# Down projection of 16 hidden tiles in seven-product blocks, on one core

## The chip, the cores and the metric

The kernel runs on one core of a Trainium2 chip. The metric is the device time of one execution in microseconds. The kernel before takes 649.57 us (median of 3 runs, 649.49 to 649.74).

## The reference

Two groups of rows, 512 of a new stream and 64 of a running one, go through one layer of a hybrid encoder: a state-space part and a latent-attention part side by side, an output projection, then a dense SwiGLU network. The change touches only the last of these:

```python
x = x + jnp.concatenate([y_ssd, o], axis=-1) @ p['w_out']
hf = rmsnorm(x, p['norm_ffn'])
x = x + (jax.nn.silu(hf @ p['w_gate']) * (hf @ p['w_up'])) @ p['w_down']
...
y_prompt = rmsnorm(xp, norm_final)
```

All values are float32. The model width is 1024, the hidden width of the SwiGLU network is 2816, and the 576 rows of both groups share the weights.

## The kernel before

The data is held transposed: channels on the 128 partitions, the 576 rows along the free axis. The model width is 8 tiles of 128 channels (`x2[0]` to `x2[7]`), the hidden width 22 tiles. A product runs over 288 rows (`TH`), half of them.

**Precision.** Every float32 operand is split into a high part in a format that TensorE multiplies at its full rate and a low part that is the rest: ScalarE writes the high part (`act.copy`), VectorE the low one (a subtraction), see `split_weights` and `split_scaled`. A product is then three: high x high, high x low, low x high.

**Gate and up, `gu_weights`, `gu_steps`, `gu_first`.** For one hidden tile f the gate and up products form a 2 x 2 block scheme: two row halves on one side, gate and up on the other, even and odd channel tiles as the inner pair. Seven block products take the place of eight. This needs sums of the weights (four additions of 512 columns on VectorE: `s1`, `s2`), three splits of 1024 columns and one of 512 (`a22`), and sums of the activations, which `x_operands` makes once. The seven products are the steps `m1` to `m7`; they accumulate in three PSUM banks `x`, `y`, `z`. `m1` is copied by ScalarE into `gl` and added to `y` by VectorE in `m2`. The steps `m4` and `m3` of one tile are issued after `m1` of the next (`late`). `finish` applies silu, multiplies gate and up into `u`, and splits `u` into `prod[f]`.

**Down, `down`, `down_terms`, `down_half`.** The hidden tiles are cut by `CUTS` into parts 0-4, 5-9, 10-13, 14-17 and 18-21. After the first tile of a part the part before goes through `down`: for each of the 8 output tiles and each half of the rows, its hidden tiles are multiplied by their weights in one PSUM bank, and VectorE adds the bank to `x2[t]`. In the first part `x2[t]` is multiplied by `Ri` before, the inverse of the norm's factor per row, so that the norm can be left to the end. The last part goes through the tail of the kernel, with the final norm.

**What sets the order.** Every engine's instructions are issued in an order written out by hand in `ISSUE`, a list of places for each engine. What moves between engines goes by semaphores. Buffers come from rotating pools: `wpool` (8) for raw weights and their sums, `w2pool` (10) for split weights, `tpool` (7) for temporaries such as `g` and `u`, PSUM banks by tag (`sc` 3, `pp` 3, `hm` 2). SP's queue loads all weights.

Of the kernel before, what the change touches and what calls it, by code (L numbers as in the profile page):

```python
# [11 lines left out]
F32 = mybir.dt.float32  # L12
F32R = mybir.dt.float32r
AF = mybir.ActivationFunctionType
ALU = mybir.AluOpType
# [4 lines left out]
P = 128  # L20
# [3 lines left out]
T = TP + TS  # L24
# [11 lines left out]
UPW = 3 + TP + 3 + TS  # L36
LAST = 18


# [15 lines left out]
def hybrid_layer_kernel(ctx: ExitStack, tc: tile.TileContext, a, o):  # L55
# [49 lines left out]
    def wslot(wp, name, dt=F32):  # L105
        return wp.tile([P, 1024], dt, tag="w", name=name)
# [26 lines left out]
    def wk(w, k, m=P):  # L133
        return tuple(z[:, k * m : (k + 1) * m] for z in w)
# [646 lines left out]
    fz = midp.tile([P, 4, T], F32, tag="xsd", name="fz")  # L781
    ss2, ss3 = fz[:, 0], fz[:, 1]
    R2, R2h = R1, R1h
# [22 lines left out]

    def gu_weights(f):

        r1, r2, s1, s2 = (wslot((w2pool, wpool)[f > 0], f"gu{f}_{z}") for z in range(4))
        sp.dma_start(r2, a["w_gu"][f, :, 1])  # L810
        gu_dma.append(sp.dma_start(r1, a["w_gu"][f, :, 0]).ins)
        l, r = (lambda z: z[:, :512]), (lambda z: z[:, 512:])
        dve.tensor_tensor(l(s1), l(r2), r(r2), ALU.add)
        dve.tensor_tensor(l(s2), l(r2), l(r1), ALU.subtract)
        dve.tensor_tensor(r(s1), l(s1), l(r1), ALU.subtract)
        dve.tensor_tensor(r(s2), r(r1), r(s1), ALU.subtract)
        a22 = wslot(w2pool, f"gu{f}_a22", F32R)
        act.copy(l(a22), r(r2))
        out = {"A22": (l(a22), r(a22))}
        for names, w in (("A11", "A12"), r1), (("S1", "S2"), s1), (("S3", "S4"), s2):  # L820
            w = split_weights(w, f"gu{f}_{names[0]}", wp=w2pool)
            for i, n in enumerate(names):
                out[n] = tuple(z[:, 512 * i : 512 * i + 512] for z in w)
        dve.tensor_tensor(r(a22), r(r2), l(a22).bitcast(F32), ALU.subtract)
        return out

    w_gu, squared, gu_dma = {}, [], []

    def square(t):
# [20 lines left out]
    def block_product(ps, w, i, kps=KPS, first=True, last=True, onto=False):  # L850

        n, xi = PRODUCTS[i - 1]
        for kp in kps:
            (whi, wlo), x = wk(w[n], kp), xops[kp][:, :, xi]
            for j, (p, q) in enumerate(((whi, x[:, 0]), (whi, x[:, 1]), (wlo, x[:, 0]))):
                pe.matmul(  # L856
                    ps, p, q, start=not onto and first and kp == kps[0] and j == 0,
                    stop=onto or (last and kp == kps[-1] and j == 2), skip_group_check=onto,
                )
# [4 lines left out]

    prod, Ri = {}, fz[:, 2]
    HC = [slice(hf * TH, (hf + 1) * TH) for hf in range(2)]

# [34 lines left out]
    def finish(f, g, u):  # L902
        act.activation(g, g, AF.Silu)
        dve.tensor_tensor(u, u, g, ALU.mult)
        s = slot(cpool, "c", f"pr{f}")
        split_scaled(s, u, None)
        prod[f] = hilo(s)

    def gu_steps(f):
# [7 lines left out]
        def m1():  # L917
            block_product(x, w, 1)
            act.copy(gl, x)

# [8 lines left out]
        def m2():  # L929
            block_product(y, w, 2)  # L930
            dve.tensor_tensor(gl, y, gl, ALU.add)
            dve.tensor_tensor(gl, gl, R2[:, :TH], ALU.mult)

# [14 lines left out]

    wout[0] = w2pool

    def down_terms(fs, t):
# [10 lines left out]
    def down(fs):  # L962

        for t in range(KT):
            terms = down_terms(fs, t)
            for hf, cols in enumerate(HC):
                ps = fbank(("hm", "sc", "pp")[(2 * t + hf) % 3], f"ps_d{fs[0]}_{t}")
                down_half(ps, terms, cols)
                if fs[0] == 0:
                    dve.tensor_tensor(x2[t][:, cols], x2[t][:, cols], Ri[:, cols], ALU.mult)  # L970
                dve.tensor_tensor(x2[t][:, cols], ps, x2[t][:, cols], ALU.add)
# [167 lines left out]
def issue_in_order(tc, nc):  # L1139
# [25 lines left out]
1190-1192 1227 1193-1198 1291-1297 1199-1201 1228 1202-1204 1286-1288 1207-1223 1318-1319 1224-1226 1298-1317  # L1165
1330-1333 1342-1343 1348-1355 1344-1347 1320-1329 1334-1341 1356-1463 1572 1464-1499 1575 1500-1523 1581-1582
1524-1554 1573-1574 1555-1558 1560-1571 1559 1583 1578-1580 1599-1601 1620 1584-1586 1605-1607 1626 1576-1577
1596-1598 1590-1592 1611-1613 1632-1634 1621 1587-1589 1608-1610 1602-1604 1623-1624 1593-1595 1614-1616 1635-1637
1629-1631 1617-1619 1638 1627-1628 1647 1622 1641-1643 1658 1656 1653-1655 1648 1625 1644 1659 1639-1640 1649-1651
1645-1646 1660-1669 1657 1682 1652 1694-1705 1683-1693 1670-1681 1730-1741 1706-1710 1718-1729 1711-1717 1754-1765  # L1170
1742-1753 1766-1777 1790-1801 1778-1789 1802-1825 1850 1862-1873 1838-1839 1826-1837 1840-1849 1851-1861 1874-1909
1922-1932 1910-1921 1934 1946-1957 1933 1935-1945 1958-1969 1982-1993 1970-1981 1994-2030 2042-2065 2093-2094
2031-2041 2095-2096 2078-2091 2097-2106 2066-2077 2108-2114 2107 2092 2115-2117 2123-2137 2118-2122 2138
""",
# [11 lines left out]
365 336 325 337 321 331 333 366 341 340 338 332 334 346 345 342 335 339 344 349 352 358 343 350 377 359 347 351 368  # L1186
353 360 354 361 356 355 348 357 369-373 376 374 390 375 382 378 383-384 389 379 385-387 380 397 405 381 388 391 394
393 398 395 392 399 401 420 396 402-403 400 406 404 408 407 462 412 409-410 417 464 414 418 416 413 421 411 423 422
419 424-425 428 426-427 415 431 429 432-433 430 463 434 438 436 435 437 442 465 439 443 441 440 466 444 451 446 467
452 468 453 447 454-455 469 473 456 475 477 448 457 474 478 476 458 472 488 470 479 481 445 489-490 449 492 480 471  # L1190
495 491 538 450 485 459 493 487 460 494 482 500 507 503 486 505 461 497 508 504 506 502 510 496 501 518 509 483
519-520 570 521 484 548 515 555 511 522-523 517 524 516 545 526 512 498 537 525 527 513 499 542 528-529 514 532 565
547 573 563 533 560 552 543 557 562 577 530 540 558 539 568 579 550 534 541 531 580 575 553 544 549 535 578 546 551
567 572 554 588 556 584 589-590 559 581 561 591 564
""",
# [8 lines left out]
230 225 272 237-239 236 245 251 246 252 248 278 247 255 254 249-250 232 257-259 256 261 253 262-264 268-270 260  # L1204
265-267 273-276 284 277 280-282 285 293 287 283 279 286 288 291 289 302 290 292 294-296 330 298 300 297 301 303-304
299 305-307 309-310 308 312 331 311 316-317 313 315 314 318 332 319 333 320 322 321 337-338 323-325 334 336 335 326
339 327 341 340 346 344 347 345 348-350 328 355-356 329 353-354 357 359 358 342-343 364 362 365-366 363 367-368 351
375 352 376 371 360 372 369 361 370 377-380 373 381-386 390 374 391 387 389 392 388 394 393 399 397 400 395 398 401
396 402-403 408-409 406 404 407 405 410-412 417-418 413 415-416 414 419-421 428-429 422 424-425 423 430-432 426
433-439 443 427 444 440 442 445 441 447 446 452 450 453 448 451 454 449 455-456 461-462 457 459-460 458 463-465  # L1210
472-473 466 468 467 469 474-477 470 478 471 479-483 487-488 484 486 489 485 491 490 496 494 497 492 495 498 493
499-500 505-506 501 503-504 502 507-509 516-517 510 512 511 513 518-521 514 522 515 523-527 531-532 528 530 533 529
535 534 540 538 541 536 539 542 537 543-544 552-553 547 545 548 546 554-555 549-551 556
""",
    "POOL": """
0-3 7 18 28 4 8 5 9 6 10 26-27 11 29 12-17 20-22 19 23-25 31 30 32-42 53 55 57 59 54 56 58 60 43-52 61-73
# [3 lines left out]
83 70 74 67 69 68 71 78 80 88 73 75 72 66 89 77 76 82 86 90-92 87 93 100 103 101-102 104-105  # L1220
""",
# [100 lines left out]
```

## Time and profile before

| | |
|---|---|
| median of 3 runs | 649.57 us |
| span of the profiled execution | 647.9 us |
| TensorE (PE) busy | 639.4 us, 4747 products |
| VectorE (DVE) busy | 510.1 us |
| ScalarE (ACT) busy | 338.3 us |
| GpSimd (POOL) busy | 43.2 us |
| DMA | 63.22 MB, mean 98 GB/s |

The profiled execution's own time is not among the runs; its span runs from its first to its last instruction. The feed-forward stage begins near 250 us, the old down projections are pieces of the chain such as 321.90, 409.55, 485.67 and 555.78 us, and the last part with the final norm begins near 606 us. In a row, L856 is the seven-product scheme, L958 the plain down projection, L112 and L113 the two halves of a weight split, L813 to L816 the weight sums. The rows give busy time, the mean length of one instruction, and the idle time of the engine in front of it with what ended it.

### The profile page before, as it was taken

What the parts mean: (1) busy time and instruction counts of PE and PEld (TensorE: products, weight loads), DVE (VectorE), ACT (ScalarE), POOL (GpSimd) and SP (SyncE); (2) the same over time, 40 slices, a digit from 0 to 9 for tenths busy, and PEclk for the clock granted to TensorE, in tenths of its full rate; (3) what the DMA queues carried; (4) which work ended last, traced back from release to release, by engine and by line L of the source; (5) the groups of instructions that cost most, each with busy time, mean ns of one, the idle gap of its engine ahead of it and who ended that gap; (6) DMA issues with size and microseconds to landing.
All of it is one profiled execution on the core that took longest, in us unless ns stands there. A gap on an engine that the chain in (4) does not pass through costs nothing.

```text
span 647.9 us, 11907 instructions
## 1 busy us (share of the span) xinstructions
PE 639.4 (99%) x4747; PEld 613.0 (95%) x4747; DVE 510.1 (79%) x932; ACT 338.3 (52%) x629; POOL 43.2 (7%) x79
## 2 busy tenths in 40 slices
PE   9999999999999999999999999999999999999996
PEld 9799999886887899999999999999999999999995
DVE  6999986999767699999895876866767676966555
ACT  7645425879666467745523455234533254335364
POOL 1422131101100000000000000000000000000022
PEclk9999999999999999999999999999999999999998
DMA  9521273313220221233322133122223223231004
GB/s 317 192 82 46 64 208 119 111 52 122 111 71 33 99 98 66 78 119 109 120 96 98 66 102 126 67 72 75 83 98 126 70 82 105 75 130 66 1 1 147
DMA packets 26151, 63.22 MB, mean 98 GB/s; under 512 B 3418, under 2 KB 10088, under 8 KB 25840
## 3 DMA queue, kind: packets, MB, share of 16 engines
q1 hardware_dynamic: 24560, 60.77, 28.0%
q0 software_dynamic: 816, 1.13, 0.7%
q8 instruction: 37, 0.61, 0.4%
q10 hardware_dynamic: 720, 0.57, 0.3%
q14 instruction: 18, 0.15, 0.1%
HBM read 58.03 MB, written 3.30 MB: 95 GB/s over the span
## 4 chain that ended last, share of the span: by engine, by line
PE 92%; DVE 4%; issue 1%; ACT 1%; DMA 1%; POOL 0%; POOLq 0%; DVEq 0%; ACTq 0%
PE ps_x L856 21%; PE ps_d L958 18%; PE ps_z L856 10%; PE ps_o L447 8%; PE ps_in L128 8%; PE ps_y L856 5%; PE ps_z L447 4%; PE ps_l L958 3%; PE ps_first L128 2%; PE ps_p L856 2%; PE sc L661 2%; PE pv L708 1%; PE ptp L683 1%; PE ps_v L594 1%; DVE mx L644 1%
## 5 line engine op out<-in xcount | busy, mean ns | idle before, releaser
L958 PE MATMUL ps_d<-pr,wh_d 128*128 128x288 f32 x576 | 115.6, 295 | 0.0
L856 PE MATMUL ps_x<-xop,wh_gu_S 128*128 128x288 f32 x504 | 101.5, 295 | 0.0
L958 PEld LDWEIGHTS ps_d<-pr,wh_d 128*128 128x128 f32 x576 | 92.6, 188 | 0.0
L958 PE MATMUL ps_d<-pr,wl_d 128*128 128x288 f32 x288 | 84.7, 295 | 0.0
L856 PEld LDWEIGHTS ps_x<-xop,wh_gu_S 128*128 128x128 f32 x504 | 80.8, 188 | 0.0
L856 PE MATMUL ps_x<-xop,wl_gu_S 128*128 128x288 f32 x252 | 74.3, 295 | 0.0
L112 ACT CAST wh_gu_S<-gu 128x1024 fp32r<-128x1024 f32 x44 | 46.2, 1050 | 39.9 <-PE ps_d L958 18.5
L113 DVE TENSOR_TENSOR wl_gu_S<-gu,wh_gu_S 128x1024 fp32r<-128x1024 f32 x44 | 53.8, 1223 | 9.0 <-PE ps_d L958 6.7
L958 PEld LDWEIGHTS ps_d<-pr,wl_d 128*128 128x128 f32 x288 | 54.1, 188 | 0.0
L856 PEld LDWEIGHTS ps_x<-xop,wl_gu_S 128*128 128x128 f32 x252 | 47.3, 188 | 0.0
L128 PE MATMUL ps_in<-xs,wh_in 128*128 128x288 f32 x256 | 45.4, 298 | 0.0
L112 ACT CAST wh_d<-wr_d 128x640 fp32r<-128x640 f32 (+1 forms) x32 | 21.5, 673 | 45.6 <-PE ps_x L856 20.4
L128 PEld LDWEIGHTS ps_in<-xs,wh_in 128*128 128x128 f32 x256 | 37.8, 189 | 0.2
L856 PE MATMUL ps_z<-xop,gu_a 128*128 128x288 f32 x252 | 37.5, 295 | 0.0
L856 PE MATMUL ps_y<-xop,wh_gu_A 128*128 128x288 f32 x168 | 35.4, 295 | 0.0
L856 PE MATMUL ps_z<-xop,wh_gu_S 128*128 128x288 f32 x168 | 35.2, 297 | 0.0
L113 DVE TENSOR_TENSOR wl_d<-wr_d,wh_d 128x640 fp32r<-128x640 f32 (+1 forms) x32 | 24.1, 756 | 13.7 <-PE ps_x L856 8.6
L856 PEld LDWEIGHTS ps_z<-xop,gu_a 128*128 128x128 f32 x252 | 34.9, 189 | 0.0
L856 PE MATMUL ps_x<-xop,wh_gu_A 128*128 128x288 f32 x168 | 34.7, 297 | 0.0
L112 ACT CAST wh_gu_A<-gu 128x1024 fp32r<-128x1024 f32 x22 | 23.1, 1050 | 21.2 <-PE ps_x L856 13.1
L113 DVE TENSOR_TENSOR wl_gu_A<-gu,wh_gu_A 128x1024 fp32r<-128x1024 f32 x22 | 27.0, 1227 | 6.9 <-PE ps_d L958 4.1
L1054 POOL TENSOR_TENSOR fz<-fz,sq 128x320 f32<-128x320 f32 x3 | 2.6, 882 | 445.7 <-ACT sq L1049 445.7
(337 smaller groups left out, 1646.9 us busy)
## 6 DMA issues: line engine op xcount, KB each, us to landing
gu<-in_w_gu SPq DMA_DIRECT2D x44, 512.0 KB, 3.7
wr_d<-in_w_down SPq DMA_DIRECT2D x16, 320.0 KB, 3.0
wr_in<-in_w_in SPq DMA_DIRECT2D x8, 512.0 KB, 5.9
wr_out<-in_w_out SPq DMA_DIRECT2D x8, 512.0 KB, 3.2
wr_d<-in_w_down SPq DMA_DIRECT2D x16, 256.0 KB, 2.6
cumb<-cumD SPq DMA_DIRECT2D x5, 512.0 KB, 4.3
x<-in_xT SPq DMA_DIRECT2D x2, 1152.0 KB, 6.5
wr_z<-in_w_in SPq DMA_DIRECT2D x4, 512.0 KB, 4.4
```

Of the source, the lines that this page charges most:

```text
L112: act.copy(hi, raw)
L113: dve.tensor_tensor(lo, raw, hi.bitcast(F32), ALU.subtract)
L128: pe.matmul(ps[:m, hf, :n], w, x[:, hf * n : (hf + 1) * n], start=start and k == 0 and i == 0, stop=stop and k == last and i == 2,)
L447: pe.matmul(ps[:, :n], w, x[:, cols], start=k == 0 and i == 0, stop=k == len(terms) - 1 and i == 2,)
L594: pe.matmul(ps[:n], l, r, start=j == 0, stop=j == 2)
L644: dve.tensor_reduce(mx[:, j : j + 1], s, AX, ALU.max, negate=True)
L661: pe.matmul(s[:, :nk], qs[:, j, q0 : q0 + P], ks[:, j, :nk], start=True, stop=True)
L683: pe.transpose(pp[:, k : k + P], prs[p, i][:, j, b * P : b * P + P], ident)
L708: pe.matmul(pv[64 * j : 64 * j + 64, b * P :], V[b][:, h * HD : (h + 1) * HD], pts[p, b, j], start=b == 0, stop=True, skip_group_check=b > 0,)
L856: pe.matmul(ps, p, q, start=not onto and first and kp == kps[0] and j == 0, stop=onto or (last and kp == kps[-1] and j == 2), skip_group_c ...
L958: pe.matmul(ps, w, x[:, cols], start=first and k == 0 and i == 0, stop=last and k == len(terms) - 1 and i == 2,)
L1054: pool.tensor_tensor(ss3[:, parts[0]], ss3[:, parts[0]], z, ALU.add)
```

## The change

The hidden tiles are cut into parts 0-1, 2-5, 6-9, 10-13, 14-17 and 18-21. Parts 0-1 and 18-21 stay plain. The four parts between go through the seven-product scheme for the down projection too: pairs of output tiles, pairs of hidden tiles and the two row halves form the blocks. Each part is done in two calls of `down_blocks`, each for four output tiles, one behind each of the first two hidden tiles of the next part. `gu_weights` becomes `block_weights`, which both stages use, with its sums on VectorE; `pair` makes the sums and splits of the activations for two hidden tiles. In both stages `m1` is copied by ScalarE from its bank into the bank of `m2`, which accumulates on it. Of each pair of output tiles, the even one is added by VectorE from PSUM; the odd one is copied to buffers `B` and `C` by ScalarE and added to `x2` by two accumulating DMAs from GpSimd's queue. The multiplication of `x2` by `Ri` moves from VectorE (16 of 288 columns) to GpSimd (8 of 576). `ss3` gets a pool of its own, and the five lists of `ISSUE` are written anew from the feed-forward stage on.

```diff
+BLOCKS = tuple(range(2, LAST + 1, 4))
...
     def gu_weights(f):
+        return block_weights(*(a["w_gu"][f, :, i] for i in range(2)), f"gu{f}", lambda z: z.rearrange("p (e b m) -> e p b m", e=2, m=P))
+    def down_weights(f, h):
+        src = a["w_down"][4 * h : 4 * h + 4, :, f * P : f * P + 512].rearrange("(t i) k c -> i k t c", i=2)
+        return block_weights(src[0], src[1], f"db{f}_{h}", lambda z: z.rearrange("p (b e m) -> e p b m", e=2, m=P))
...
+    def block_weights(src1, src2, name, blocks):
+        n = len(gu_dma)
+        sums = dve
+        r2, r1, s1, s2 = (wslot((w2pool, wpool)[n > 0], f"{name}_{z}") for z in range(4))
...
+        sums.tensor_tensor(l(s1), l(r2), r(r2), ALU.add)
+        sums.tensor_tensor(l(s2), l(r2), l(r1), ALU.subtract)
+        sums.tensor_tensor(r(s1), l(s1), l(r1), ALU.subtract)
+        sums.tensor_tensor(r(s2), r(r1), r(s1), ALU.subtract)
+        a22 = wslot(w2pool, f"{name}_a22", F32R)
         act.copy(l(a22), r(r2))
...
     def finish(f, g, u):
         act.activation(g, g, AF.Silu)
         dve.tensor_tensor(u, u, g, ALU.mult)
+        if BLOCKS[0] <= f < LAST:
+            return paired(f, u)
...
         def m1():
             block_product(x, w, 1)
-            act.copy(gl, x)
+            act.copy(y, x)
...
         def m2():
-            block_product(y, w, 2)
-            dve.tensor_tensor(gl, y, gl, ALU.add)
-            dve.tensor_tensor(gl, gl, R2[:, :TH], ALU.mult)
+            block_product(y, w, 2, onto=True)
+            dve.tensor_tensor(gl, y, R2[:, :TH], ALU.mult)
...
+    def pair(f):
...
+        x, y = (halves(tmp(f"pv{f}_{i}")) for i in range(2))
+        dve.tensor_tensor(x[:, 0], e[:, 1], e[:, 0], ALU.subtract)
+        dve.tensor_tensor(x[:, 1], e[:, 1], d[:, 1], ALU.subtract)
+        dve.tensor_tensor(y[:, 0], d[:, 1], x[:, 0], ALU.subtract)
+        dve.tensor_tensor(y[:, 1], d[:, 0], y[:, 0], ALU.subtract)
+        for z, v in ((a11, e[:, 0]), (own, d), (t13, x), (t24, y)):
+            zr = z.bitcast(F32R)
+            act.copy(zr[:, 0], v)
+            dve.tensor_tensor(zr[:, 1], v, z[:, 0], ALU.subtract)
...
+    def down_steps(fs, w, h, p):
+        t = 4 * h + 2 * p
+        qs = blocks[(fs[0] - BLOCKS[0]) // 2 :][:2]
+        x, y, z = fbank("hm", f"ps_dx{fs[0]}_{t}"), fbank("sc", f"ps_dy{fs[0]}_{t}"), fbank("pp", f"ps_dz{fs[0]}_{t}")
+        B, C = (tmp(f"d{i}{fs[0]}_{t}") for i in "bc")
...
+        def add_to(t, v):
+            pool.dma_start(x2[t], v, accum_op=ALU.add)
+        def m1():
+            sums(x, 1)
+            act.copy(y, x)
+        def m6():
+            sums(x, 6, True)
+            act.copy(B[:, :TH], x)
+        def m7():
+            sums(z, 7)
+            act.copy(C[:, TH:], z)
+        def m2():
+            sums(y, 2, True)
+            dve.tensor_tensor(x2[t][:, :TH], y, x2[t][:, :TH], ALU.add)
+        def m5():
+            sums(x, 5, True)
+            act.copy(B[:, TH:], x)
+            add_to(t + 1, B)
+        def m4():
+            sums(z, 4, True)
+            act.copy(C[:, :TH], z)
+            add_to(t + 1, C)
+        def m3():
+            sums(x, 3, True)
+            dve.tensor_tensor(x2[t][:, TH:], x, x2[t][:, TH:], ALU.add)
+        return m1, (m4, m3), (m6, m7, m2, m5)
+    def down_blocks(fs, h, late):
+        w = down_weights(fs[0], h)
+        for p in range(2):
+            first, rest, middle = down_steps(fs, w, h, p)
+            for step in (first, *late, *middle):
+                step()
+            late = rest
+        return late
...
                 down_half(ps, terms, cols)
-                if fs[0] == 0:
-                    dve.tensor_tensor(x2[t][:, cols], x2[t][:, cols], Ri[:, cols], ALU.mult)
+                if hf == 0:
+                    pool.tensor_tensor(x2[t], x2[t], Ri, ALU.mult)
                 dve.tensor_tensor(x2[t][:, cols], ps, x2[t][:, cols], ALU.add)
-    CUTS = (0, 5, 10, 14, LAST, FT)
+    CUTS = (0, *BLOCKS, FT)
...
-            if f == part[0] and f:
+            if f == part[0] == BLOCKS[0]:
                 for step in late:
                     step()
                 late = ()
                 down(prev)
+                fz2.append(midp.tile([P, 4, T], F32, tag="xsd", name="fz2"))
+            elif f in part[:2] and f > BLOCKS[0] + 3:
+                late = down_blocks(prev, f - part[0], late)
+                if f == part[1] and f < LAST:
+                    late += (lambda f=f: pair(f),)
```

More of the change, by code (lines that the diff above doesn't have):

```diff
@@ L820, in gu_weights @@
         for names, w in (("A11", "A12"), r1), (("S1", "S2"), s1), (("S3", "S4"), s2):
-            w = split_weights(w, f"gu{f}_{names[0]}", wp=w2pool)
-            for i, n in enumerate(names):
-                out[n] = tuple(z[:, 512 * i : 512 * i + 512] for z in w)
+            hi, lo = split_weights(w, f"{name}_{names[0]}", wp=w2pool)
+            for i, z in enumerate(names):
+                out[z] = tuple((blocks if w is r1 else halves_of)(y)[i] for y in (hi, lo))
         dve.tensor_tensor(r(a22), r(r2), l(a22).bitcast(F32), ALU.subtract)
@@ L827, in hybrid_layer_kernel @@
     w_gu, squared, gu_dma = {}, [], []
+    held, blocks, fz2 = {}, [], []
     def square(t):
@@ L949, in hybrid_layer_kernel, with paired @@
     wout[0] = w2pool
+    def paired(f, u):
+        held[f] = u
+        k = (f - BLOCKS[0]) % 4
+        if k == 3 or f == BLOCKS[0] + 1:
+            pair(f)
+    def pair(f):
+        k = (f - BLOCKS[0]) % 4
+        e, d = halves(held.pop(f - 1)), halves(held.pop(f))
+        a11 = fz2[0][:, k // 2].rearrange("p (a n) -> p a n", a=2)
+        own, t13, t24 = (
+            (fz2[0][:, 2:4] if k == 3 and z == "o" else slot(cpool, "c", f"pb{f}{z}")).rearrange("p a (b n) -> p a b n", b=2)
+            for z in "oxy"
+        )
+        x, y = (halves(tmp(f"pv{f}_{i}")) for i in range(2))
[7 more added lines that the diff above has]
+            dve.tensor_tensor(zr[:, 1], v, z[:, 0], ALU.subtract)
+        q = {XB11: a11.bitcast(F32R)}
+        for z, names in ((own, (XB21, XB22)), (t13, (XT1, XT3)), (t24, (XT2, XT4))):
+            for i, n in enumerate(names):
+                q[n] = z.bitcast(F32R)[:, :, i]
+        blocks.append(q)
@@ new lines, in down_steps, with sums @@
+    def down_steps(fs, w, h, p):
[3 more added lines that the diff above has]
+        B, C = (tmp(f"d{i}{fs[0]}_{t}") for i in "bc")
+        def sums(ps, i, onto=False):
+            n, xi = PRODUCTS[i - 1]
+            for k, q in enumerate(qs):
+                whi, wlo = (z[:, 2 * p + k] for z in w[n])
+                o = q[xi]
+                for j, (l, r) in enumerate(((whi, o[:, 0]), (whi, o[:, 1]), (wlo, o[:, 0]))):
+                    pe.matmul(
+                        ps, l, r, start=not onto and k == 0 and j == 0, stop=onto or (k == 1 and j == 2), skip_group_check=onto,
+                    )
+        def add_to(t, v):
[24 more added lines that the diff above has]
+        return m1, (m4, m3), (m6, m7, m2, m5)
@@ L1174 @@
+4286-4403
 """,
```

161 lines of the change are left out of this document (123 added, 38 removed).

## The prediction

> **What bounds the kernel now.** I read the engine totals first, then the strip over the span, then the chain of waits, then the stretches, and only then single instructions.
>
> ```profile
> PE 639.4 (99%) x4747; PEld 613.0 (95%) x4747; DVE 510.1 (79%) x932; ACT 338.3 (52%) x629; POOL 43.2 (7%) x79
> ...
> DVE  6999986999767699999895876866767676966555
> ...
> PEclk9999999999999999999999999999999999999998
> ```
>
> TensorE is busy for the whole span at a full granted clock, but a busy PE could still be an inefficient one, so the chain and the stretches have to say whether it waits.
>
> ```profile
> 485.67 22.13 PE ps_d L958 x167
> ```
>
> ```profile
> core 0: us, PE busy (x) PEld busy (x) DVE busy (x) ACT busy (x) POOL busy (x), PEclk, DMA share, GB/s
> 274.00:306.00 32.00, 32.00 (x243) 32.00 (x242) 30.81 (x53) 16.83 (x25) 0.00 (x0) 1.00 0.34 112
> 507.80:577.90 70.10, 70.10 (x531) 70.10 (x530) 51.63 (x85) 29.21 (x45) 0.00 (x0) 1.00 0.28 91
> ```
>
> The first row is a piece of the chain: 167 products of the old down projection in 22.13 us without a gap, 0.1325 us each. The second and third are stretches of the feed-forward: PE holds 32.00 of 32.00 us and 70.10 of 70.10 us. So in this stage the number of products sets the time, and an edit is worth its products as long as the other engines keep TensorE fed. VectorE is what may fail: 96% busy in 274 to 306 us, 74% in one period of four hidden tiles (507.80 to 577.90).
>
> **What is removed from TensorE.** The old down projection of 18 tiles has 18 x 8 output tiles x 2 halves x 3 terms = 864 products. Tiles 0 and 1 keep 96. The other 16 become 4 groups x 2 halves of the output x 2 pairs of output tiles x 7 block products x 2 pairs of hidden tiles x 3 terms = 672. That is 96 fewer, 96 x 0.1325 = **12.7 us**. The number of products of the gate and up stage does not change.
>
> **What VectorE does instead.** These rows (by shape, 245 to 632 us) carry the terms that go or stay:
>
> ```profile
> L113 DVE TENSOR_TENSOR wl_gu_S<-gu,wh_gu_S 128x1024 fp32r<-128x1024 f32 x42 | 51.4, 1223 | 9.0 <-PE ps_d L958 6.7 <-ACT wh_gu_S L112 1.8
> L971 DVE TENSOR_TENSOR x<-ps_d,x 128x288 f32<-128x288 f32 x64 | 28.7, 453 | 3.9 <-PE ps_d L958 3.8
> L144 DVE TENSOR_TENSOR pr<-u,pr 128x576 fp32r<-128x576 f32 x22 | 16.5, 752 | 1.5 <-ACT pr L142 1.5
> L113 DVE TENSOR_TENSOR wl_d<-wr_d,wh_d 128x512 fp32r<-128x512 f32 x16 | 11.0, 689 | 7.8 <-PE ps_x L856 5.7 <-PE ps_y L856 1.9
> L931 DVE TENSOR_TENSOR g<-ps_y,g 128x288 f32<-128x288 f32 x21 | 9.6, 458 | 21.5 <-PE ps_y L856 21.5
> L970 DVE TENSOR_TENSOR x<-x,fz 128x288 f32<-128x288 f32 x16 | 7.0, 455 | 0.0
> ```
>
> Back to back, an instruction costs less than its row's length, since the next one starts before it ends:
>
> ```profile
> 276.76 0.70 DVE L814 TENSOR_TENSOR gu<-gu,gu 128x512 f32<-128x512 f32 x1
> 277.36 0.71 DVE L815 TENSOR_TENSOR gu<-gu,gu 128x512 f32<-128x512 f32 x1
> ...
> 282.74 0.78 DVE L899 TENSOR_TENSOR g<-g,R 128x576 f32<-128x576 f32 x1
> 283.40 1.25 DVE L113 TENSOR_TENSOR wl_gu_S<-gu,wh_gu_S 128x1024 fp32r<-128x1024 f32 x1
> 284.54 0.48 DVE L936 TENSOR_TENSOR u<-ps_x,u 128x288 f32<-128x288 f32 x1
> 284.90 0.78 DVE L904 TENSOR_TENSOR u<-u,g 128x576 f32<-128x576 f32 x1
> ```
>
> From start to start: 0.60 us for 512 columns, 0.66 for 576, 1.14 for 1024, 0.36 for 288. One weight set (four sums and one half split of 512, three splits of 1024) is 5 x 0.60 + 3 x 1.14 = 6.4 us. A hidden tile before: the set, five additions and factors of 288, the product u*g and the split of `pr`, 6.4 + 1.8 + 0.66 + 0.66 = 9.5. Four of them and one `down` of four tiles (8 x 0.60 + 16 x 0.36 = 10.6) make 48.8; the stretch shows 51.63, as rows that stand alone run their whole length.
>
> After: a hidden tile is 6.4 + 4 x 0.36 + 0.66 = 8.5 (`m2` no longer adds the first product, and `pr` is not split). Each `pair` is four sums and a split of 288 and three splits of 576, 5 x 0.36 + 3 x 0.66 = 3.8. Each `down_blocks` is a full weight set and four additions, 6.4 + 1.4 = 7.9. A period: 4 x 8.5 + 2 x 3.8 + 2 x 7.9 = 57.4 us beside 6 x 84 products x 0.1325 = 66.8 us of TensorE: 86%, or 91% after scaling by 51.63/48.8. VectorE gets more work than before but stays below TensorE, and the trace shows TensorE whole at 96%. I cost this at nothing outside one place.
>
> **The tight place** is hidden tiles 1 to 7. There, weights are ready just in time already:
>
> ```profile
> 274.90 1.23 DVE L113 TENSOR_TENSOR wl_gu_S<-gu,wh_gu_S 128x1024 fp32r<-128x1024 f32 x1
> ...
> 276.83 0.29 PE L856 MATMUL ps_z<-xop,wl_gu_S 128*128 128x288 f32 x1
> ```
>
> This split ends at 276.13 and is used at 276.83: 0.7 us ahead. I added up both engines in the changed kernel's issue order (by the durations above) against the old order, from that anchor. For the first split of tile 2, TensorE comes to it 3.05 us earlier than in the old order and VectorE only 1.86 us earlier, 1.2 us less of a margin that was 0.9: -0.3, so a stall of **0.3 us**. Then the plain `down` of tiles 0 and 1 gives VectorE room: from tile 2's last split to tile 3's first one, 15.5 us of VectorE beside 18.4 of TensorE, a margin of 3 us. From there to the end of tile 7's weights VectorE needs 54.9 us while TensorE needs 56.0 (98%): what is lost before is not won back there, and the margin grows by 1 to 2 us only. After tile 8 it grows steadily.
>
> **GpSimd beside VectorE.** In exactly that room the change puts eight multiplications of x2 by Ri, 128x576, on GpSimd: in the issue order they can start when Ri's second half is written, which VectorE does right behind tile 2's last split. Nearest rows:
>
> ```profile
> L1103 POOL TENSOR_TENSOR fz<-fz,sq 128x256 f32<-128x256 f32 x4 | 2.9, 736 | 6.4 <-ACT sq L1098 6.2
> L1054 POOL TENSOR_TENSOR fz<-fz,sq 128x320 f32<-128x320 f32 x3 | 2.6, 882 | 445.7 <-ACT sq L1049 445.7
> ```
>
> ```profile
> 625.58 0.89 POOL L1054 TENSOR_TENSOR fz<-fz,sq 128x320 f32<-128x320 f32 x1 [0.29 <-ACT sq L1049]
> ...
> 626.29 0.53 DVE L1059 TENSOR_TENSOR sq_last<-sq_last,sq 128x320 f32<-128x320 f32 x1 [0.25 <-ACT sq L1049]
> ...
> 627.56 0.49 DVE L1059 TENSOR_TENSOR sq_last<-sq_last,sq 128x320 f32<-128x320 f32 x1 [0.18 <-ACT sq L1049]
> ```
>
> By the first two, 64 columns cost 0.146 us, so 576 cost 0.88 + 256 x 0.146/64 = 1.47 us, eight 11.7 us. The other three show the same VectorE instruction with and without a GpSimd one under it: 0.53 against 0.49. Had it been held, it would have started 0.53 - 0.49 late, at 626.33, 0.14 before the GpSimd row ends at 626.47. One overlap of 0.18 us proves little, but it fits a hold until shortly before GpSimd's end. From below the cost is nothing (the 0.04 may be noise; a gain is excluded, since GpSimd does not help VectorE's queue beyond the 16 L970 rows already left out). From above each of the eight holds VectorE for 1.47 - 0.14 = 1.33 us: 10.6. I take 60% of it, the share of VectorE's work in those 15.5 us that reads two operands from SBUF (splits, sums, u*g; the rest reads PSUM): 6.4 us, less the margin of 3: **3.4 us** on TensorE.
>
> The Trainium skill, "SBUF — State Buffer", section "Who interferes with whom", speaks against this edit: a VectorE instruction with two SBUF inputs contends with a GpSimd instruction that reads SBUF, and whichever comes second is blocked for the whole instruction. The rows just shown agree as far as 0.04 us can; by the full rule the time would be that of the second rival below.
>
> **ScalarE.** These rows price its additions:
>
> ```profile
> L112 ACT CAST wh_gu_S<-gu 128x1024 fp32r<-128x1024 f32 x42 | 44.1, 1050 | 38.6 <-PE ps_d L958 18.5 <-PE ps_x L856 13.4 <-PE ps_y L856 4.2
> L919 ACT COPY g<-ps_x 128x288 f32<-128x288 f32 x21 | 8.4, 399 | 17.3 <-PE ps_x L856 17.3
> ```
>
> A `down_blocks` costs about 3.5 casts of 1.05 and ten copies of 0.40, 7.7 us in 11.1 of TensorE; a hidden tile with its share of `pair` about 7. It has room. The copy from bank to bank is not in the trace; its neighbours are the 0.40 us copies into SBUF, and between `m1` and `m2` lie four other block products (over 3 us in a down block), which would cover several times that: nothing.
>
> **The accumulating DMAs** (32 of 128x576, 288 KB, from GpSimd's queue) have no twin in the trace:
>
> ```profile
> qs<-rrp POOLq DMA_DIRECT2D x16, 36.0 KB, 2.2
> out_ckvT<-ckf POOLq DMA_DIRECT2D x1, 288.0 KB, 4.9
> ```
>
> So 2.2 us from below and, with the destination read as well as written, twice 4.9 = 9.8 from above; I take 4, nearer to the row of the same size, though it goes to memory outside the core. Who waits: B and C are two of seven `tpool` buffers, and ScalarE's next `u` copy waits for the first B of each second half-block, issued 3 to 4 us of products before, with about 1.5 us more until TensorE needs that copy. At 4 us: nothing. GpSimd's queue has nothing else behind these waits until the last norm, two tiles later. DMA share there is 0.28.
>
> **Sum** for the profiled execution: span 647.9 - 12.7 + 0.3 + 3.4 = 638.9. Its own time lies 1.7 us above the span if it is like the median of the runs, 649.57; the same 1.7 gives **640.6 us**.
>
> **Rivals.**
> First, GpSimd's work costs VectorE nothing: 649.57 - 12.7 + 0.3 = 637.2. For it: the one overlap cost 0.04 us, which may be noise. Against it: the start it implies fits a hold.
> Second, the hold is complete, or VectorE idles a few per cent where it must reach 98%: 10.6 - 3 + 0.3 = 7.9 us lost, 644.8; with 4% idling of 54.9 us on top, 647. For it: VectorE never lacks work there. Against it: PSUM readers pass.
> Third, slower: the accumulating DMAs are slow. From some 5 us upward ScalarE is held at `u`, the casts queue behind it, and TensorE stops; once per group, four times. At 9.8 us that is about 4 x 4.5 = 18 us, so 649.57 - 12.7 + 18 = 655 without the GpSimd cost; it turns into a loss from about 8 us per DMA. For it: nothing in the trace adds while it transfers. Against it: 4.9 us for the same bytes on the same queue.
> The Trainium skill, "DMA: Bandwidth & Descriptors", section "Anatomy of one DMA — SWDGE (gpsimd) path", fits such a DMA as 2.0 us plus bytes over 436 GB/s, an estimate of 2.7 us here; by it the third rival never starts, but no run here shows an accumulating one.
> Fourth, the change does not do what it says: an output block that needs eight products after all would leave 649.6. The loops issue 672; I give it almost nothing.
>
> **How the numbers follow.** Forecast 0.40, first rival 0.27, second 0.19, third 0.13, fourth 0.01. A measurement tells 0.2% (1.3 us) from no change. All but the third and fourth lie over that below 649.57; a part of the second and third lands near it: faster 0.82, same 0.05, slower 0.13. The range runs from just under the first rival, 636.4, to 650.5, which takes in the second and the mild half of the third.
>
> **What would show it.** Right: L958-like rows fall from 864 to 96 plain and 672 block products at 0.1325 us each; VectorE 85 to 92% busy per period with PE whole; PE gaps only around 277 to 300 us, 3 to 4 us in sum, behind VectorE splits, with GpSimd rows of about 1.5 us beside VectorE rows that are longer or start late. Wrong: no gap there (first rival), PE gaps once per group behind ScalarE with DMA as the releaser (third), or a PE that waits for VectorE throughout tiles 8 to 19, which would make my account of VectorE wrong.

## The result: slower by 0.5%, and the profile after

The changed kernel takes 652.92 us (median of 5 runs, 651.09 to 654.62), the kernel before 649.57 beside it (649.45 to 650.02): ratio 1.0047, 95% interval 1.003 to 1.0064. The forecast was 640.6 us, with a range up to 650.5. The profiled execution of after took 651.58 us, span 649.9.

The engine totals and part of the strip of after, to be laid beside those of before:

```profile
PE 634.3 (98%) x4651; PEld 604.3 (93%) x4651; DVE 546.9 (84%) x967; ACT 380.4 (59%) x733; POOL 84.8 (13%) x119
...
DVE  6999986999767699999999898978898699785664
...
PEclk9999999999999999979999999999999899999998
...
PE 77%; DVE 12%; DMA 5%; ACT 3%; issue 2%; POOL 0%; POOLq 0%; DVEq 0%; ACTq 0%
```

TensorE has its 96 products fewer (4651 against 4747), but it is no longer whole: the last row, the chain of work that ended last by engine, gives it 77% (before: 92%) and VectorE 12% (before: 4%). The granted clock dips in the 18th and the 32nd slice. The stretches say how much is lost where. First after, then the run in which both suspects, GpSimd's multiplications and the accumulating DMAs, are left out (e4 below):

```profile
core 0: us, PE busy (x) PEld busy (x) DVE busy (x) ACT busy (x) POOL busy (x), PEclk, DMA share, GB/s
274.00:306.00 32.00, 29.84 (x198) 28.96 (x197) 29.97 (x46) 13.98 (x24) 13.62 (x8) 0.89 0.36 115
480.00:520.00 40.00, 37.92 (x269) 37.09 (x269) 30.62 (x49) 22.04 (x41) 4.31 (x5) 0.96 0.43 109
360.10:430.20 70.10, 69.70 (x523) 69.34 (x522) 61.01 (x94) 41.03 (x73) 7.92 (x10) 1.00 0.54 138
```

```profile
274.00:306.00 32.00, 32.00 (x241) 31.73 (x240) 28.47 (x55) 16.08 (x27) 0.00 (x0) 1.00 0.37 117
480.00:520.00 40.00, 39.75 (x296) 39.11 (x295) 33.57 (x53) 24.33 (x44) 0.00 (x0) 1.00 0.26 82
360.10:430.20 70.10, 70.10 (x528) 69.93 (x528) 60.92 (x96) 41.15 (x71) 0.00 (x0) 1.00 0.28 92
```

Two places carry most of the loss that the trace shows. In 274 to 306 us after does 198 products instead of 241: 43 x 0.1325 = 5.7 us. In 480 to 520 us it does 269 instead of 296: 3.6 us. In the period between, little is lost, and VectorE is 87% busy (61.01 of 70.10).

**The first place.** GpSimd's row, VectorE's rows beside it, and TensorE's waits, from the timeline of after:

```profile
277.90 13.62 POOL L1079 TENSOR_TENSOR x<-x,fz 128x576 f32<-128x576 f32 x8 [99.73 <-issue]
```

```profile
278.40 1.21 DVE L114 TENSOR_TENSOR wl_d<-wr_d,wh_d 128x256 fp32r<-128x256 f32 x1
279.54 1.98 DVE L920 TENSOR_TENSOR u<-u,g 128x576 f32<-128x576 f32 x1
282.56 0.50 DVE L114 TENSOR_TENSOR wl_d<-wr_d,wh_d 128x256 fp32r<-128x256 f32 x1 [1.04 <-ACT wh_d L113]
282.99 1.96 DVE L145 TENSOR_TENSOR pr<-u,pr 128x576 fp32r<-128x576 f32 x1
284.87 0.45 DVE L961 TENSOR_TENSOR g<-ps_x,R 128x288 f32<-128x288 f32 x1
...
291.99 0.74 DVE L145 TENSOR_TENSOR pr<-u,pr 128x576 fp32r<-128x576 f32 x1
```

```profile
282.29 0.70 PE L1067 MATMUL ps_d<-pr,wh_d 128*128 128x288 f32 x2 [0.67 <-ACT pr L143]
285.01 1.57 PE L1067 MATMUL ps_d<-pr,wh_d 128*128 128x288 f32 x5 [1.49 <-DVE pr L145]
```

The split of `pr` takes 1.96 us under GpSimd's work and 0.74 us behind it. Every VectorE instruction with two operands in SBUF is longer there, by 0.5 to 1.2 us (that at 282.56 by 0.07 only); those that read PSUM (284.87) keep their 0.45 us. The eight such rows between 278.4 and 292 us are together 7.1 us longer than the same rows of e4. The same `pr` is what TensorE waits for.

**The second place.** VectorE's rows with their waits, TensorE's, and SP's issues of the weight loads:

```profile
498.40 0.69 DVE L829 TENSOR_TENSOR gu<-gu,gu 128x512 f32<-128x512 f32 x1 [2.59 <-DMA gu<-in_w_gu]
...
507.14 0.69 DVE L827 TENSOR_TENSOR gu<-gu 128x512 f32<-128x512 f32 x1 [1.84 <-DMA gu<-in_w_gu]
507.75 0.45 DVE L953 TENSOR_TENSOR u<-ps_x,u 128x288 f32<-128x288 f32 x1
511.35 0.69 DVE L829 TENSOR_TENSOR gu<-gu,gu 128x512 f32<-128x512 f32 x1 [3.14 <-DMA gu<-in_w_gu]
```

```profile
508.26 0.53 PE L871 MATMUL ps_x<-xop,wh_gu_S 128*128 128x288 f32 x2 [1.76 <-DVE u L953]
```

```profile
490.86 0.34 SPq L824 DMA_DIRECT2D gu<-in_w_gu  x1
492.60 0.34 SPq L825 DMA_DIRECT2D gu<-in_w_gu  x1
501.36 0.33 SPq L824 DMA_DIRECT2D gu<-in_w_gu  x1
503.83 0.33 SPq L825 DMA_DIRECT2D gu<-in_w_gu  x1
```

VectorE stands 7.6 us behind weight loads (2.59 + 1.84 + 3.14), and the evacuation that TensorE needs (507.75) stands behind one of them in its queue. The load issued at 501.36 is there at 507.14, 5.8 us later; that of 503.83 at 511.35, 7.5 us later. The median such load of before took 3.7 (bytes, median us from issue to landing, from the page of before):

```profile
gu<-in_w_gu SPq DMA_DIRECT2D x44, 512.0 KB, 3.7
```

The 7.6 us are not all the accumulating DMAs' doing. Without them (e3 below) VectorE still waits 4.6 us for two loads at the same place in the order:

```profile
497.86 0.69 DVE L846 TENSOR_TENSOR gu<-gu,gu 128x512 f32<-128x512 f32 x1 [1.66 <-DMA gu<-in_w_gu]
508.78 0.69 DVE L846 TENSOR_TENSOR gu<-gu,gu 128x512 f32<-128x512 f32 x1 [2.93 <-DMA gu<-in_w_gu]
```

These loads were issued at 492.98 and 503.28 and took 4.9 and 5.5 us. So the DMAs add about 3.0 us to VectorE's wait here. The rest is there without them, and e4, where VectorE waits 4.0 us here, loses little by it (296 products).

### The profile page after: what moved, and what is told of

Its sections match the earlier page's. It is cut to its first block, busy times and chain, and to the rows that moved or that the text cites. A ratio compares the mean times of both kernels' runs of the same rounds, so it can differ in the third digit from the quotient of the medians.

```text
span 649.9 us, 12004 instructions
## 1 busy us (share of the span) xinstructions
PE 634.3 (98%) x4651; PEld 604.3 (93%) x4651; DVE 546.9 (84%) x967; ACT 380.4 (59%) x733; POOL 84.8 (13%) x119
## 4 chain that ended last, share of the span: by engine, by line
PE 77%; DVE 12%; DMA 5%; ACT 3%; issue 2%; POOL 0%; POOLq 0%; DVEq 0%; ACTq 0%
PE ps_x L871 16%; PE ps_o L448 8%; PE ps_z L871 8%; PE ps_in L129 8%; PE ps_dx L1012 6%; PE ps_z L448 4%; PE ps_y L871 4%; PE ps_dz L1012 3%; DMA gu<-in_w_gu 2%; PE ps_first L129 2%; PE ps_d L1067 2%; PE ps_p L871 2%; PE ps_l L1067 2%; PE ps_dy L1012 2%; PE sc L662 2%
## 5 line engine op out<-in xcount | busy, mean ns | idle before, releaser
L871 PE MATMUL ps_x<-xop,wh_gu_S 128*128 128x288 f32 x504 | 113.8, 298 | 1.8 <-DVE u L953 1.8
L871 PEld LDWEIGHTS ps_x<-xop,wh_gu_S 128*128 128x128 f32 x504 | 84.5, 190 | 2.4 <-DVE u L953 2.2
L871 PE MATMUL ps_x<-xop,wl_gu_S 128*128 128x288 f32 x252 | 74.0, 297 | 0.0
L871 PE MATMUL ps_z<-xop,gu_a 128*128 128x288 f32 x252 | 48.6, 301 | 0.0
L871 PEld LDWEIGHTS ps_x<-xop,wl_gu_S 128*128 128x128 f32 x252 | 47.6, 190 | 0.0
L1017 POOL DMA_DIRECT2D x<-db x16 | 14.9, 929 | 225.1 <-ACT db L1037 99.2
L871 PEld LDWEIGHTS ps_z<-xop,gu_a 128*128 128x128 f32 x252 | 39.6, 194 | 0.1
L871 PE MATMUL ps_x<-xop,wh_gu_A 128*128 128x288 f32 x168 | 39.5, 296 | 0.2 <-ACT wh_gu_A L113 0.2
L871 PE MATMUL ps_z<-xop,wh_gu_S 128*128 128x288 f32 x168 | 39.2, 297 | 0.0
L871 PE MATMUL ps_y<-xop,wh_gu_A 128*128 128x288 f32 x168 | 38.4, 295 | 0.0
L871 PEld LDWEIGHTS ps_x<-xop,wh_gu_A 128*128 128x128 f32 x168 | 28.4, 188 | 0.5 <-ACT wh_gu_A L113 0.4
L448 PE MATMUL ps_o<-cat_y,wh_out 128*128 128x288 f32 x128 | 28.5, 310 | 0.0
L871 PEld LDWEIGHTS ps_z<-xop,wh_gu_S 128*128 128x128 f32 x168 | 28.2, 188 | 0.1
L871 PEld LDWEIGHTS ps_y<-xop,wh_gu_A 128*128 128x128 f32 x168 | 28.0, 188 | 0.3 <-ACT ps_y L937 0.3
L129 PE MATMUL ps_in<-xs,wl_in 128*128 128x288 f32 x128 | 27.5, 297 | 0.0
L448 PE MATMUL ps_o<-cat_o,wh_out 128*128 128x288 f32 x128 | 27.1, 296 | 0.0
```

The source lines that it names most:

```text
L129: pe.matmul(ps[:m, hf, :n], w, x[:, hf * n : (hf + 1) * n], start=start and k == 0 and i == 0, stop=stop and k == last and i == 2,)
L448: pe.matmul(ps[:, :n], w, x[:, cols], start=k == 0 and i == 0, stop=k == len(terms) - 1 and i == 2,)
L871: pe.matmul(ps, p, q, start=not onto and first and kp == kps[0] and j == 0, stop=onto or (last and kp == kps[-1] and j == 2), skip_group_c ...
L1017: pool.dma_start(x2[t], v, accum_op=ALU.add)
```

## The experiments

Each experiment changes the kernel after; "against before" is its median less that of the kernel before, measured beside it. Where instructions were left out or put in, their line numbers are 17 to 19 higher (L888 for L871).

| run | median us | against before | ratio, 95% interval |
|---|---|---|---|
| after | 652.92 | +3.35 | 1.0047, 1.003 to 1.0064 |
| e1: no Ri multiplications | 645.65 | -4.05 | 0.9935, 0.9923 to 0.9947 |
| e2: Ri on VectorE | 652.04 | +2.34 | 1.0037, 1.0023 to 1.0052 |
| e3: no accumulating DMAs | 646.49 | -3.21 | 0.9943, 0.993 to 0.9955 |
| e4: neither | 639.09 | -10.61 | 0.9843, 0.983 to 0.9855 |
| e5: plain copies | 649.92 | +0.08 | 1.0001, 0.9993 to 1.001 |
| e6: sums later | 652.80 | +2.96 | 1.0042, 1.003 to 1.0054 |
| e7: Ri in VectorE's gaps | 652.00 | +2.16 | 1.0027, 1.0017 to 1.0038 |
| e8: e6 and e7 | 651.10 | +1.26 | 1.0022, 1.001 to 1.0034 |
| e9: gaps, order mended | 648.25 | -1.58 | 0.998, 0.9969 to 0.9992 |
| e10: both orders mended | 647.43 | -2.40 | 0.996, 0.9945 to 0.9975 |
| e12: buffers free early | 651.96 | +2.09 | 1.0032, 1.002 to 1.0045 |
| e13: e10 without the DMAs | 642.37 | -7.50 | 0.9886, 0.9871 to 0.9901 |

### Two suspects, one at a time and together

e1 and e4 leave out GpSimd's multiplications, e3 and e4 the 32 DMAs:

```diff
-                if hf == 0:
-                    pool.tensor_tensor(x2[t], x2[t], Ri, ALU.mult)
...
         def add_to(t, v):
-            pool.dma_start(x2[t], v, accum_op=ALU.add)
```

e1: 

> The changed kernel with GpSimd's eight multiplications of x2 by Ri left out (that part of the computation is missing). Theory, two separate losses: GpSimd's multiplications at 278 to 295 us stretch VectorE's instructions with two SBUF operands and cost 5.6 us there, the accumulating DMAs cost the rest elsewhere. It expects 647 to 648 us, eviction-free instructions such as the 128x256 weight split back at 0.42 us, and the late weight loads near 500 us still there. Rival, VectorE's own load is the bound, whoever multiplies: 651 to 653 us, with the same idle time of TensorE moved a little later.

e3: 

> The changed kernel with the 32 accumulating DMAs left out (the additions to the odd output tiles are missing); ScalarE still copies the sums out of PSUM. Theory, the accumulating DMAs slow SP's weight loads, VectorE's queue stands behind late weight sums, TensorE idles and its granted clock falls: 647 to 649 us, median weight load back at about 3.7 us, runs within 1 us of each other instead of 3.5. Rival, the loads are late because VectorE frees the weight buffers late: 652 to 653 us, loads near 500 us still over 5 us.

e4: 

> Both left out, the multiplications by Ri and the accumulating DMAs. Theory, the two losses add: 641 to 643 us, that is 652.9 less 5.6 less about 4.7; if nothing else was lost, 637. Rival, VectorE's load is the bound: 650 us or more.

The multiplications cost 3.35 + 4.05 = 7.4 us, the DMAs 3.35 + 3.21 = 6.6, both together 3.35 + 10.61 = 14.0: the prices add, so these are two separate losses. The split that took 1.21 us takes 0.42 in e4. The rival of VectorE's load "whoever multiplies" is not yet out: e1 multiplies nowhere. All three came out below what was expected: I had put the prices at 5.6 and about 4.7 us. The rival for e3, that the weight buffers come free late, is out as the price of the DMAs: 6.6 us come back without them, and the median load is 3.9 us. But it holds in part: near 500 us a load of e3 still takes 5.5 us and VectorE waits up to 2.9 us for it. Nor did the spread of e3's runs, 2.4 us, shrink to 1 as I expected. e4 also shows that the rest of the change does nearly all that it should: 10.6 us faster than before.

### Is it GpSimd, or the time at this place?

```diff
-                    pool.tensor_tensor(x2[t], x2[t], Ri, ALU.mult)
+                    dve.tensor_tensor(x2[t], x2[t], Ri, ALU.mult)   # ahead of the first addition to x2[t]
```

> The changed kernel with the eight multiplications by Ri on VectorE (128x576 each), directly ahead of the first addition to that tile. VectorE gets about 8 x 0.75 = 6.0 us of work and loses the stretch of about 8 us. Theory, GpSimd's hold costs VectorE more than the work itself: 648 to 651 us, faster than the changed kernel (652.9). Rival, VectorE's load is the bound: 654 to 659 us, slower than the changed kernel.

652.04 us: neither. VectorE's own 6 us cost as much as GpSimd's hold, within what can be told apart. So the hold is real, yet the choice of GpSimd is not all that was wrong: the 6 to 7 us have no room in this order on either engine. GpSimd's multiplications at another place were not run. Where VectorE has room showed in e4's trace, where it idles 3.0 us between 279 and 290 us, in four gaps in front of instructions that wait for ScalarE, TensorE or a load. In e2 the multiplications stand behind these gaps. e7 puts the first four into them (the lists of numbers told in words):

```diff
 VectorE's order
+x2[0] *= Ri
 split of wl_d0_1, of pr0
+x2[1] *= Ri
 ...
+x2[2] *= Ri                  (ahead of a sum of tile 3)
+x2[3] *= Ri                  (ahead of the split of wl_d0_4)
 ...
+x2[4] to x2[7] *= Ri         (between the additions)
 ...
-sums of tiles 4 and 5, first split of tile 4
 additions to x2[4] to x2[7]
+sums of tiles 4 and 5, first split of tile 4
```

> The changed kernel with the eight multiplications by Ri on VectorE, the first four placed where VectorE stood idle without them (about 3.0 us between 279 and 290 us in the run without both), the others between the additions, with sums and splits of tiles 4 and 5 put behind them. Theory, what was lost there is VectorE's order and time at this one place, and idle time takes up half of the 6 us: 648 to 650 us. Rival, VectorE has no time at all to give until tile 7: 652 us, as with the multiplications directly ahead of the additions.

652.00 us. By the number the rival holds; the trace says otherwise. Up to 303 us TensorE lost little, and then it waited for what I had put behind:

```profile
306.57 0.40 PE L888 MATMUL ps_x<-xop,wl_gu_A 128*128 128x288 f32 x1 [1.76 <-DVE wl_gu_A L131]
314.22 0.40 PE L888 MATMUL ps_z<-xop,wh_gu_S 128*128 128x288 f32 x1 [1.90 <-ACT wh_gu_S L130]
```

That was my order. e9 puts that split and the first sums of tile 4 ahead again:

> As the run with the multiplications by Ri in VectorE's gaps, but with the split of tile 4's first weights and its sums put back ahead: there TensorE had waited 1.8 and 1.9 us for just these at 306 and 314 us. Theory, VectorE's time at this place can be given by order: 648 to 650 us. Rival, VectorE is full and each order only moves the wait: 651 to 652.5 us, with about 5 us less of products than without the multiplications, at another place before tile 8.

648.25 us, 4.9 us less than after, and faster than before. One stretch of four kernels, after, e2, e9 and e4:

```profile
274.00:320.00 46.00, 43.84 (x302) 42.84 (x301) 42.38 (x67) 20.42 (x34) 13.62 (x8) 0.93 0.32 104
```
```profile
274.00:320.00 46.00, 42.30 (x305) 40.57 (x304) 41.63 (x76) 20.25 (x34) 0.00 (x0) 1.00 0.31 104
```
```profile
274.00:320.00 46.00, 44.53 (x329) 43.52 (x327) 44.28 (x80) 21.85 (x36) 0.00 (x0) 1.00 0.36 115
```
```profile
274.00:320.00 46.00, 46.00 (x346) 45.68 (x345) 40.89 (x75) 23.62 (x39) 0.00 (x0) 1.00 0.41 127
```

302 products with GpSimd, 305 with VectorE in a row, 329 in the gaps, 346 without. VectorE is 44.28 us busy in e9 and 41.63 in e2, with the same work on it: it had the time, in another order.

### How the DMAs cost time

e5 turns the additions into copies of the same bytes. e12 keeps the additions but lets them read a constant tile, so that ScalarE's buffers are free at once.

```diff
 e5
-            pool.dma_start(x2[t], v, accum_op=ALU.add)
+            pool.dma_start(x2[t], v)
 e12
-            pool.dma_start(x2[t], v, accum_op=ALU.add)
+            pool.tensor_tensor(v[:, :1], v[:, :1], v[:, T - 1 :], ALU.add)
+            pool.dma_start(x2[t], R1, accum_op=ALU.add)
```

e5: 

> The changed kernel with the 32 accumulating DMAs turned into plain copies of the same bytes to the same tiles (the odd tiles are overwritten instead of added to). If the reading and adding at the destination is what costs: 647 to 648 us, as with the DMAs left out (646.5). If it is the transfers themselves, the bytes that they carry beside the weight loads: 651 to 653 us, as in the changed kernel (652.9).

e12: 

> The changed kernel with the 32 accumulating DMAs at their places, but reading a constant tile instead of the buffers that ScalarE fills (the odd tiles get wrong additions): ahead of each a GpSimd instruction of one column (it waits for ScalarE as the DMA did, and after it the buffer is free). The transfers stay, the holding of the buffers goes. Theory, the DMAs cost time by slowing the weight loads: 651.5 to 653 us. Rival, by holding ScalarE's buffers: 647 to 650 us.

The DMA issues of after and then of e5 (bytes each, median us from issue to landing):

```profile
gu<-in_w_gu SPq DMA_DIRECT2D x44, 512.0 KB, 4.1
x<-db POOLq DMA_DIRECT2D x16, 288.0 KB, 5.6
x<-dc POOLq DMA_DIRECT2D x16, 288.0 KB, 4.3
```

```profile
gu<-in_w_gu SPq DMA_DIRECT2D x44, 512.0 KB, 4.0
x<-db POOLq DMA_DIRECT2D x16, 288.0 KB, 4.0
x<-dc POOLq DMA_DIRECT2D x16, 288.0 KB, 2.4
```

e5 falls between its two theories: plain copies give back 3.3 of the 6.6 us. So about half of the price is the adding and half the transfer. e12 gives back 1.3 us, which the intervals hardly tell from nothing; the buffers that ScalarE waits for are at most a small part. The trace of after has one such wait:

```profile
594.70 0.40 ACT L945 COPY u<-ps_z 128x288 f32<-128x288 f32 x1 [1.00 <-DMA x<-db]
```

GpSimd's issues and the transfers do not lengthen VectorE's instructions either: between 330 and 600 us the splits of 1024 columns (`wl_gu_S`) take 1.221 us on the mean in after and 1.222 in e3. What is left is what the transfers do to the loads beside them. That is argued by exclusion and from the late loads near 500 us, not shown by a run with the loads alone changed, such as one with more buffers for weights.

If VectorE's queue behind late sums passes the lateness on, another order should help. e6 puts the sums of tiles 16 and 17 behind the evacuations and splits that stood behind them (in words again):

```diff
 VectorE's order from 495 us
-sums of 16 (2), u14, sum of 16, x2 += ps_dx, split of db a22, sum of 16, x2 += ps_dy, x2 += ps_dx, split of db A11
+x2 += ps_dx, split of db a22, x2 += ps_dy, x2 += ps_dx, split of db A11, u14, sums of 16 (2)
-g15, split of db S1, sum of 17, u15, sum of 17, u15, split of db S3
+g15, split of db S1, sum of 16, u15, sum of 16, u15, split of db S3
 ...
+sums of 17
```

e6: 

> The changed kernel with one change in VectorE's order alone, near 495 to 513 us: the weight sums of tiles 16 and 17 stand behind the evacuations and the splits of the down weights that stood behind them. Theory, the accumulating DMAs cost time because VectorE's queue stands behind sums that wait for late loads (7.6 us of VectorE's time there): about 3 us of their 6.4 come back, 649 to 650.5 us. Rival, the weights themselves come too late, whatever the order: 652 to 654 us, the wait goes to TensorE's own weights.

e8: 

> The two changes of order together, multiplications by Ri on VectorE in its gaps and the sums of tiles 16 and 17 later; it computes the reference. If both theories hold: 645 to 647 us, faster than both kernels. If neither: 652 us.

e6: 652.80 us, the rival's number. Its windows and waits for TensorE:

```profile
500.00:520.00 20.00, 18.64 (x140) 18.32 (x139) 14.38 (x23) 9.98 (x18) 2.58 (x3) 1.00 0.56 134
520.00:580.00 60.00, 58.71 (x439) 58.01 (x439) 53.40 (x85) 33.54 (x57) 6.05 (x7) 1.00 0.51 131
```
```profile
PE ps_x L871 <- DVE u L953: 1.4, 1, 1.4
PE ps_x L871 <- DVE wl_gu_S L114: 0.9, 1, 0.9
```

The loss had moved on: 140 products in 500 to 520 us, where after has 119, but 439 in 520 to 580 us, where after has 453. One trace tells this only roughly: at the first place, which the edit does not touch, e6's profiled execution does 187 products in 274 to 306 us and after's 198, which is 1.5 us. e8, e6 with e7, is 651.10 us: each order had a fault of its own. e10 mends both (e9's order; near 500 us the sums of 16 stand between the evacuations, and its splits ahead of tile 15's operands):

e10: 

> The same, and near 495 to 525 us VectorE's order mended once more: sums of tile 16 between the evacuations, its later splits ahead of the operands of tile 15. It computes the reference. If both orders hold: 646 to 648 us, faster than both kernels; if the waits only move: 650 to 652 us.

e13: 

> The version with both orders of VectorE mended (647.4 us), with the accumulating DMAs left out (the additions to the odd tiles are missing). If the orders gave back Ri's price alone: 641 us, the DMAs still at 6.4 us; if VectorE's later order near 500 us had taken up a part of it: 642 to 643 us. Over 639.1 us (neither Ri nor DMAs) is what the multiplications still cost.

e10: 647.43 us, faster than before by 0.25 to 0.55% and than after by 5.8 us. The stretch near 500 us, of e9 and then of e10:

```profile
480.00:520.00 40.00, 37.86 (x271) 37.13 (x270) 30.76 (x49) 22.21 (x41) 4.31 (x5) 0.96 0.44 106
```
```profile
480.00:520.00 40.00, 39.40 (x296) 39.06 (x295) 33.02 (x51) 24.57 (x45) 6.06 (x7) 1.00 0.51 124
```

It is whole again: 296 products, as without the DMAs. That is 3.3 us more than in e9's trace; between the two profiled executions (650.15 and 647.53) 2.6 us of it arrive, but e9's was 1.9 us above the median of its runs, and between the medians it is 0.8, inside the intervals. e13 tells what is left: without the DMAs the mended orders take 7.50 - 2.40 = 5.1 us less, so most of the DMAs' price was still there, in small pieces elsewhere. In 400 to 420 us e10 has 145 products and e13 153; in 580 to 600 us (e10, then e13):

```profile
580.00:600.00 20.00, 19.48 (x146) 19.01 (x145) 12.34 (x17) 10.61 (x18) 3.48 (x4) 1.00 0.63 152
580.00:600.00 20.00, 20.00 (x153) 20.00 (x152) 13.36 (x21) 11.66 (x21) 0.00 (x0) 1.00 0.22 80
```

And 10.61 - 7.50 = 3.1 us are what the multiplications in the gaps and the later sums cost together. By e13's trace 2.4 us of it lie at the multiplications (328 products in 274 to 320 us, where e4 has 346), against 7.4 for GpSimd's, and 0.8 behind the later sums (448 in 520 to 580 us, where e4 has 454).

## Why the prediction was wrong, point by point

**Products, -12.7 us: right, nearly.** e4 has the change without its two suspects. The first rival's sum, nothing lost but tile 2's 0.3 us, gave 637.2; e4 takes 639.1, 1.9 more. e4's TensorE shows only one wait of 0.3 us. Its products are a little further apart, 528 in 70.10 us where before had 531; what holds them apart was not found.

**VectorE, nothing outside the tight place: right.** 87% against the 86 to 91% worked out, with TensorE whole but for 0.4 us of 70.10. **Copy from bank to bank, nothing: right as far as shown.** It takes 0.39 us, and in the feed-forward stage a single weight load waits 0.3 us for it, and no product; alone it was not run.

**GpSimd, 3.4 us: wrong, 7.4.** The hold was well sized: 6.4 forecast, 7.1 in the rows, though each GpSimd instruction took 1.70 us (13.62/8) and not 1.47. The step that failed is "less the margin of 3". I had worked it out as VectorE's work against TensorE's between two splits, and such a margin exists: e4's idle 3.0 us. But an engine that works in order can't draw on it where it lies in front of an instruction that waits for something else. In after VectorE is held and still idles 1.04 us at 281.5 and 0.74 at 294.0, both for ScalarE: of e4's four gaps two are left, and about 1.2 us of the 3 took up hold. 7.1 less 1.2 is 5.9, near the 5.7 us of products missing there; where the rest of the 7.4 lies was not found (the profiled executions of after and e1 are 5.4 us apart). The second rival, with the whole hold, came to 7.9 us lost there, the nearest to what was measured, but by luck: it took 10.6 for the hold, 3.5 too much, and took off the same margin of 3. e9 shows what the gaps are worth once the work stands in them: 3.9 us less than e2, which has the same work on the same engine behind them, and 4.9 less than after.

The Trainium skill, "SBUF — State Buffer", section "Who interferes with whom", says that a VectorE instruction with two SBUF inputs contends with a GpSimd one that reads SBUF, and that the one that issues first has the shared ports for its whole instruction. The trace agrees that they contend, with 0.5 to 1.2 us more for nearly every such VectorE instruction and nothing for the PSUM readers; no hold is longer than 1.22 us of GpSimd's 1.70. That argument speaks against GpSimd only, and e2 shows that here the alternative cost nearly the same.

**Accumulating DMAs, nothing: wrong, 6.6 us.** The duration I took, 4 us, is near the 4.3 and 5.6 measured and inside the bounds. The step that failed is "who waits": I priced only ScalarE's wait for the buffers, the third rival's mechanism, and that is little: 1.00 us once in the trace, 1.3 us by e12. I had the DMA share of before, 0.28, and asked nothing of SP's loads, whose sums stand at the head of VectorE's queue with a lead of one load: tile 16's first load can be issued at 490.86, when tile 15's `a22` has freed its buffer, and its first sum stands at 495.13, 4.3 us later; its second load is issued at 492.60 and wanted at 495.8, 3.2 us later. Loads of 4.9 and 5.5 us, as in e3, already pass such a lead, and 5.8 to 7.5 us in after pass it by more. How the whole 6.6 us come about stays open: the trace shows 3.2 us of it near 500 us (269 products where e3 has 293), the rest in small pieces. The third rival's time, 655, was near the measured one by luck, for another reason.

**Sum.** 637.2 forecast without GpSimd's cost, 1.9 more by e4, 7.4 and 6.6 make 653.1; measured 652.9. The range was too low since its upper end counted the DMAs only by the mild half of a rival that did not happen.

## What to carry to other kernels

Where TensorE is full and another engine works at 95%, its margin is not the difference of two sums: read from the trace in front of which instruction the idle time lies, and put added work there or count the margin as nothing. When a change adds transfers, price the loads that are on the way at the same time too, by their lead (from the buffer's release to the first use), and not only who waits for the new transfers. A wait that is moved by a new order comes back at the next use; follow it for a whole period before the order is called better.

## What was not expected of the hardware

An accumulating DMA of 288 KB occupies the DMA engines more than twice as long as a plain one. GpSimd's queue in before, after and e5 (packets, MB, share of 16 engines):

```profile
q0 software_dynamic: 816, 1.13, 0.7%
```
```profile
q0 software_dynamic: 5424, 10.57, 9.3%
```
```profile
q0 software_dynamic: 3376, 10.57, 4.5%
```

The 32 transfers make 4608 packets with the addition and 2560 without, 8.6% against 3.8% of the span. The Trainium skill, "DMA: Bandwidth & Descriptors", section "Anatomy of one DMA — SWDGE (gpsimd) path", fits a DMA on this path as 2.0 us plus bytes over 436 GB/s, an estimate of 2.7 us for these bytes. Plain copies took 2.4 and 4.0 us here, accumulating ones 4.3 and 5.6.

TensorE's granted clock fell to half for some 6 to 7 us behind waits of only 0.67 and 1.49 us. Three stretches of after:

```profile
283.00:286.00 3.00, 1.51 (x8) 1.28 (x8) 3.00 (x4) 1.17 (x3) 3.00 (x2) 0.73 0.54 168
286.00:289.00 3.00, 3.00 (x14) 3.00 (x13) 3.00 (x5) 0.40 (x2) 3.00 (x3) 0.50 0.04 15
289.00:292.00 3.00, 3.00 (x17) 3.00 (x17) 3.00 (x3) 0.68 (x1) 2.51 (x2) 0.63 0.00 0
```

In e3 the same two waits, 0.70 and 1.50 us, left the clock at 1.00, and a third of 2.17 us followed. Both kernels do 198 products in 274 to 306 us. So between these two the slow clock cost nothing by itself: it filled time that TensorE would have waited for VectorE. It is no rule: e5 and e6, with the same work there and a mean clock of 0.95, do 188 and 187. Why the clock falls in one run and not in the other stays open.

The Trainium skill, "TensorE: Matmul & The Clock Gate", section "What's actually happening", puts the clock at half after at least one idle window of about 3.4 us, and says that the window runs freely, whatever the kernel does. Here it fell with no single wait that long; a window that runs freely could fall differently in the two runs, but nothing here shows it.
